# A two-layer decoder trunk: attention's transposes a slot later, logits in two banks, two steps held back at a chunk's end, the first microseconds in another order

## The chip, the cores and the metric

One core of a Trainium2 chip runs the whole program. The metric is the device time of one execution in microseconds (us). The kernel before was timed in three runs, and one more execution was profiled. The engines are TensorE (PE: matmuls and transposes, results in PSUM banks), VectorE (DVE), ScalarE (ACT), GpSimd (POOL) and SyncE (SP, which here only starts transfers).

## The reference

A batch of one, 256 tokens of width 2048, two layers, all in float32. Layer 0 is HGRN2 (a gated linear recurrence over chunks of 64 tokens), layer 1 native sparse attention (NSA) with 16 heads of 128 in 4 groups:

```python
for i in range(2):                       # x: (1, 256, 2048)
    h = rms_norm(x, g[i])
    x = x + (hgrn2_mixer(h) if i == 0 else nsa_mixer(h))
return rms_norm(x, final_gain)

# nsa_mixer, per group of 4 heads:
proj = h @ w_in                          # q, six of k and v, gate logits, z
K_cmp, V_cmp = compress_kv(...)          # 15 blocks of 32 tokens, stride 16
o = sum over b in (compressed, selected, window) of
        gate_b * softmax(q @ K_b.T + rel_bias) @ V_b
return (o * silu(z)) @ w_out
```

With 256 tokens every selection block is taken, so the selected and the window branch both see all causal keys. A head's logits for 256 queries cover 2 x 256 such keys and 15 compressed ones, for each half of the queries as far as the mask lets them.

## The kernel before, in words

**Products.** Each large product is split: an operand is cast to a rounded part `hi` (ACT, L132) and a rest `lo` (DVE, L142), and hi x hi, hi x lo and lo x hi are summed in PSUM. Weights come in pieces of 128x1024 on SP's queue into six buffers. The list `plan` holds all pieces in order, and `flush` goes through it; a chunk is a run of eight pieces whose products end in the same four PSUM banks (`mainps`). One piece is called a *slot* here: eight pairs of L173 (512 columns) and L175 (256 columns) on PE. Four more banks (`auxps`) serve everything else. At a chunk's end `take` (`gather`) copies each bank by ACT (L301) and adds its second half by DVE (L303); the next chunk's first product waits for its bank.

**Steps beside the products.** Everything else is a generator in the list `steps`. `flush` advances each of them twice a piece: once ahead of the piece's products (even steps) and once behind them (odd steps). So a step's place in the table `turns` decides where its instructions stand in each engine's queue, and each engine takes its queue in order.

**Attention.** The chunks of the NSA layer are q0, q1, q2, z0, q3, z1, z2, z3, after keys and values, and then the output product. `attend(g)` for the heads of group g starts 12g+2 slots behind q0. In a head it does: `logits` (nine matmuls on PE, Kh and Kl against qh and ql), `biased` (DVE adds the bias and takes the maxima), `exps` (ACT, with sums), `weigh` (reciprocal on DVE, scaling on ACT and DVE), `transposes` (PE, seven, in two banks), `evacuate` (ACT casts to `ph` and `pc`, DVE forms `pl`), and for every two heads `values` (PE, in two halves) and `values_out` (ACT, `ot`). `gated` multiplies z by its norm, applies SiLU (ACT, which loads a table before and after), multiplies by the attention's output and splits it into `yh` (ACT) and `yl` (DVE).

**Start.** `load_x` and `emit_load` start the loads of x and the first weights on SP. `split_x` transposes two tiles of x (PE, L326) and splits them (ACT L329, DVE L332). `setup` makes masks and tables a step at a time; its transposes of the parameter rows `prow` (L392) feed the lower bounds of the gates, which the first chunk's end needs.

Of the kernel before, what the change touches and what calls it, by code (L numbers as in the profile page):

```python
# [8 lines left out]
F32 = mybir.dt.float32  # L9
# [7 lines left out]
P = 128  # L17
# [28 lines left out]
def kernel(ctx: ExitStack, tc: tile.TileContext, x, norm_gains, final_gain, rel_bias,  # L46
# [19 lines left out]
    def aux_bank():  # L66
        return psa.tile([P, 512], F32, tag="aux", name="auxps")
# [172 lines left out]
    def start_piece(i):  # L240
        while state["hi"] <= min(i, len(plan) - 1):
            j = state["hi"]
            ch, kts, _ = plan[j]
            if ch and ch["before"]:
                ch["before"](kts)
            prefetch(j, 1)
            while state["lo"] <= j:
                emit_lo(state["lo"])
                state["lo"] += 1
            prefetch(j, 0)  # L250

    def flush():
        start_piece(2)
        finished = None
        for i, (ch, kts, last) in enumerate(plan):
            starting = ch is not None and ch["before"]
            if ch is not None:
                if finished:
                    finished()
                    finished = None  # L260
                advance()
            if not starting:
                prefetch(i, SPLIT_AHEAD)
            if ch is None:
                continue
            emit_products(i, (lambda: start_piece(i + 3)) if starting else None)
            if last and ch.get("take"):
                ch["take"](ch["ps"])
# [38 lines left out]

    sp = ctxs["start"].enter_context(tc.tile_pool(name="start", bufs=1))
    xt = sp.tile([P, 2, D], F32, name="xt")
    ssqp = sp.tile([P, 2, 4], F32, name="ssqp")  # L310
    ssq = sp.tile([P, 2], F32, name="ssq")
    junk = sp.tile([P, 512], F32, name="junk")
# [35 lines left out]
    brow = const.tile([NH, 384], F32, name="brow")  # L348
    rb = sp.tile([BUCKETS, NH], F32, name="rb")

    def setup():

        si = sp.tile([P, 32], I32, name="si")
# [22 lines left out]
        nc.vector.tensor_tensor(gt, ti, si, op=ALU.is_ge)  # L376
        xf = sp.tile([P, 32], F32, name="xf")
        nc.gpsimd.tensor_copy(xf, xi)
        yield
        yield  # L380
        cg = sp.tile([P, 7, 32], F32, name="cg")
# [2 lines left out]
        mf = sp.tile([P, 6, 32], F32, name="mf")  # L384
        nc.vector.tensor_sub(mf, cg[:, 0:6], cg[:, 1:7])
        nc.gpsimd.tensor_copy(masks, mf)
        yield
        yield
        yield
        pp = aux_bank()  # L390
        for i in range(2):
            nc.tensor.transpose(pp[:, i * P:(i + 1) * P], prow[:, i, :], ident)  # L392
# [468 lines left out]
    def attend(g):  # L861
# [4 lines left out]

        def logits(h):

            b0, b1, b2 = aux_bank(), aux_bank(), aux_bank()
            ks = [t[:, g] for t in NS["K"]]  # L870
            first = [bass.AP(tensor=k.tensor, offset=k.offset, ap=[list(k.ap[0]), [280, 2], [1, 136]]) for k in ks]
            for tt, dst, (kh, kl) in ((0, b0[:, 0:272], first), (1, b1[:, 0:272], [k[:, 8:280] for k in ks]),
                                      (1, b2[:, 0:256], [k[:, 280:536] for k in ks])):
                qh, ql = (t[:, h % 2, tt * P:(tt + 1) * P] for t in NS["q", g, h // 2])
                mm3(dst, qh, ql, kh, kl, True, True)
            l = ns.tile([P, 816], F32, tag="L", name="L", bufs=1)
            mx = ns.tile([P, 6], F32, tag="mx", name="mx")
# [4 lines left out]
            prt = ((1, b0[:, 8:136], bi[:, 128:256], l[:, 0:128]),  # L882
                   (0, b0[:, 0:7], bi[:, 159:256:16], l[:, 256:263]),
                   (2, b0[:, 136:264], bi[:, 128:256], l[:, 128:256]),
                   (4, b1[:, 0:256], bi, l[:, 304:560]),
                   (3, b1[:, 256:271], bi[:, 31:256:16], l[:, 288:303]),
                   (5, b2[:, 0:256], bi, l[:, 560:816]))
            L[h] = l, sm, prt, mx

        def biased(h):  # L890
# [75 lines left out]
        def at(slot, after, f, *a):  # L966
            turns.setdefault(2 * slot + after, []).append((f, a))

        for h in range(4):
            at(3 * h, 1, logits, h)  # L970
            at(3 * h + 1, 0, biased, h)
            at(3 * h + 1, 1, exps, h)
            at(3 * h + 2, 0, weigh, h)
            at(3 * h + 2, 1, transposes, h)
            at(3 * h + 3, 0, evacuate, h)
        for a in range(2):
            at(6 + 6 * a, 1, values, a, 0)
            at(7 + 6 * a, 1, values, a, 1)
            at(8 + 6 * a, 0, values_out, a)
        if g + 1 < G:  # L980
            for a in range(2):
                at(10, 0, get_bias, g + 1, a)
        for n in range(max(turns) + 1):
            for f, a in turns.get(n, ()):
                f(*a)
            yield

# [120 lines left out]
    residual(("x1", 4), x1_dram, *cols[4])()  # L1108

    nc.gpsimd.memset(prow, 0.0)  # L1110
    nc.gpsimd.dma_start(prow[0:48, 0, :], hgrn_lb.rearrange("a (h d) -> (a h) d", d=HD))
    nc.gpsimd.dma_start(prow[48:49, 0, :], hgrn_head_gain)
    nc.gpsimd.dma_start(prow[49:50, 0, :], phi_k_b1)
    nc.gpsimd.dma_start(prow[50:51, 0, :], phi_v_b1)
    nc.gpsimd.dma_start(prow[0:32, 1, :], nsa_pe_k[0])
    nc.gpsimd.dma_start(prow[32:64, 1, :], nsa_pe_v[0])
    nc.gpsimd.dma_start(rb, rel_bias)
    for c in range(8):
        load_x(c)
        for i in ((0, 1) if c == 0 else (c + 1,)):  # L1120
# [1 line left out]
                loaded[i] = emit_load(i)  # L1122
    state["load"] = RAW_BUFS
    gp = aux_bank()
    nc.tensor.transpose(gp[:, :32], gn, ident[:32, :32])
    nc.vector.tensor_copy(gcol, gp[:, :32])
    start_piece(0)
    for i in range(10):
        nc.tensor.transpose(gp[:, 256:256 + P], ident, ident)
    run(setup())  # L1130
    run(norm_x())
    flush()
# [32 lines left out]
```

## Time and profile before

| | us |
|---|---|
| median of 3 runs (lowest, highest) | 987.43 (986.7, 988.48) |
| the profiled execution | 988.16 |
| its span, first to last instruction | 986.3 |
| PE busy | 968.3 (98% of the span) |
| DVE busy | 658.1 (67%) |
| ACT busy | 543.7 (55%) |
| POOL busy | 52.4 (5%) |

The span is what the trace shows; the 1.9 us between it and the profiled execution's time lie around the first and the last instruction. The mean granted TensorE clock is 0.998. A busy time is a sum over the whole span; where an engine waits, and for whom, is read stretch by stretch.

### The profile page before, as it was taken

To read this page: it belongs to the slowest core of one execution; us is meant where nothing else is said; L and a number is where in the kernel's file an instruction comes from. 1 tells how busy PE (TensorE), PEld (TensorE's weight loads), DVE (VectorE), ACT (ScalarE), POOL (GpSimd) and SP (SyncE) were. 2 spreads that over 40 slices of the span, in tenths; PEclk is the share of its full clock that TensorE was granted. 3 is DMA by queue.
4 is the path that set the end of the run, shared out by engine and by line. 5 is a ranking of instruction groups with operands and counts; after the bars stand their busy time and mean duration, and the time that the engine had idled before them with its cause. 6 is when DMAs were issued, how large, how long until landed. Compare 5 with 4: busy or idle time off the path is not lost.

```text
span 986.3 us, 17479 instructions
## 1 busy us (share of the span) xinstructions
PE 968.3 (98%) x6721; PEld 836.3 (85%) x6721; DVE 658.1 (67%) x1274; ACT 543.7 (55%) x976; POOL 52.4 (5%) x154
## 2 busy tenths in 40 slices
PE   7999999999999999999999999999999999999996
PEld 6888888888888887888888898998899889888886
DVE  5778376846784678365556766455787888786654
ACT  6734563446344634455545655445777877875442
POOL 3101000100010001000011000000000000000000
PEclk9999999999999999999999999999999999999999
DMA  9555565555556555667777666574454445457662
GB/s 316 179 162 174 159 190 152 171 170 176 166 158 186 165 165 154 201 186 243 236 223 227 197 213 192 165 242 162 138 162 130 149 129 151 149 164 239 204 214 98
DMA packets 102612, 178.98 MB, mean 181 GB/s; under 512 B 6016, under 2 KB 25056, under 8 KB 102400
## 3 DMA queue, kind: packets, MB, share of 16 engines
q1 hardware_dynamic: 100512, 171.86, 56.8%
q0 software_dynamic: 1680, 5.46, 1.7%
q8 instruction: 53, 0.87, 0.4%
q10 hardware_dynamic: 336, 0.54, 0.1%
q14 instruction: 31, 0.25, 0.1%
HBM read 173.62 MB, written 4.22 MB: 180 GB/s over the span
## 4 chain that ended last, share of the span: by engine, by line
PE 92%; ACT 3%; DVE 2%; issue 1%; DMA 1%; SPq 0%; POOL 0%; DVEq 0%; POOLq 0%; ACTq 0%
PE mainps L150 40%; PE mainps L173 28%; PE mainps L175 14%; PE auxps L150 4%; PE auxps L491 2%; ACT L L900 1%; DVE lo L142 1%; DMA xt<-in_x_dram 1%; ACT hi L132 1%; PE auxps L920 1%; PE auxps L326 0%; PE auxps L502 0%; PE auxps L549 0%; PE auxps L550 0%; PE auxps L506 0%
## 5 line engine op out<-in xcount | busy, mean ns | idle before, releaser
L132 ACT CAST hi<-raw 128x1024 fp32r<-128x1024 f32 (+3 forms) x317 | 328.6, 1040 | 288.7 <-PE mainps L150 176.2
L142 DVE TENSOR_TENSOR lo<-raw,hi 128x1024 fp32r<-128x1024 f32 (+3 forms) x317 | 380.1, 1208 | 160.4 <-ACT hi L132 158.8
L173 PE MATMUL mainps<-xx,hi 128*128 128x512 f32 x1280 | 455.3, 398 | 4.1 <-DVE zs L303 3.2
L175 PE MATMUL mainps<-xx,lo 128*128 128x256 f32 x1280 | 357.6, 279 | 0.0
L173 PEld LDWEIGHTS mainps<-xx,hi 128*128 128x128 f32 x1280 | 240.8, 188 | 59.1 <-DVE zs L303 4.1
L175 PEld LDWEIGHTS mainps<-xx,lo 128*128 128x128 f32 x1280 | 241.8, 189 | 0.2
L150 PE MATMUL mainps<-hi,xx 128*128 128x512 f32 (+1 forms) x704 | 211.8, 377 | 0.0
L150 PEld LDWEIGHTS mainps<-hi,xx 128*128 128x128 f32 x704 | 128.4, 188 | 23.2
L150 PE MATMUL mainps<-lo,xx 128*128 128x512 f32 (+1 forms) x352 | 130.8, 372 | 0.0
L150 PE MATMUL mainps<-hi,yh 128*128 128x512 f32 (+1 forms) x288 | 105.9, 368 | 0.0
L150 PE MATMUL mainps<-hi,yl 128*128 128x512 f32 (+1 forms) x288 | 105.3, 366 | 0.0
L150 PE MATMUL mainps<-lo,yh 128*128 128x512 f32 (+1 forms) x288 | 105.3, 366 | 0.0
L150 PEld LDWEIGHTS mainps<-lo,xx 128*128 128x128 f32 x352 | 66.1, 188 | 10.1
L150 PEld LDWEIGHTS mainps<-hi,yl 128*128 128x128 f32 x288 | 54.3, 189 | 8.7
L150 PEld LDWEIGHTS mainps<-lo,yh 128*128 128x128 f32 x288 | 54.4, 189 | 8.6
L150 PEld LDWEIGHTS mainps<-hi,yh 128*128 128x128 f32 x288 | 54.4, 189 | 8.5
L900 ACT ACTIVATE L<-L,mx 128x128 f32<-128x128 f32 (+1 forms) x96 | 37.5, 393 | 23.4 <-DVE mx L895 23.4
L303 DVE TENSOR_TENSOR zs<-mainps,zs 128x256 f32<-128x256 f32 x48 | 18.7, 420 | 13.2 <-ACT zs L301 12.2
L533 POOL COPY ST<-S 32x128 f32<-32x128 f32 x32 | 14.6, 455 | 226.4 <-DVE S L526 225.2
L893 DVE CUSTOM_DVE_ANT_0 L<-auxps,bias 128x128 f32<-128x128 f32 (+1 forms) x96 | 22.0, 291 | 3.4 <-PE auxps L150 2.7
L938 DVE TENSOR_TENSOR pl<-auxps,ph 128x512 fp32r<-128x512 f32 (+1 forms) x32 | 17.3, 554 | 9.8 <-ACT ph L934 8.4
L564 DVE SCALAR_TENSOR_TENSOR y<-auxps,rs,sz 128x128 f32<-128x128 f32 x32 | 9.0, 344 | 22.2 <-POOL rs L79 22.2
(243 smaller groups left out, 859.3 us busy)
## 6 DMA issues: line engine op xcount, KB each, us to landing
raw<-in_hgrn_w_in_dram SPq DMA_DIRECT2D x127, 512.0 KB, 3.9
raw<-in_nsa_w_in_dram SPq DMA_DIRECT2D x104, 512.0 KB, 3.8
raw<-in_hgrn_w_out_dram SPq DMA_DIRECT2D x32, 512.0 KB, 4.8
raw<-in_nsa_w_out_dram SPq DMA_DIRECT2D x32, 512.0 KB, 4.4
raw<-in_nsa_w_in_dram SPq DMA_DIRECT2D x10, 420.0 KB, 3.4
xt<-in_x_dram SPq DMA_DIRECT2D x8, 256.0 KB, 8.4
raw<-in_x_dram SPq DMA_DIRECT2D x4, 512.0 KB, 4.0
x_dram<-x POOLq DMA_DIRECT2D x4, 512.0 KB, 6.2
```

What stands on the lines that cost most here:

```text
L132: nc.scalar.copy(hi[:, :m], raw[:, :m])
L142: nc.vector.tensor_sub(lo[:, :m], raw[:, :m], hi[:, :m].bitcast(F32))
L150: nc.tensor.matmul(dst, a, b, start=first and n == 0, stop=last and n == 2, skip_group_check=True)
L173: nc.tensor.matmul(ps, hv[:, fs], xx[:, k].rearrange("p a t -> p (a t)"), start=k == 0, stop=False, skip_group_check=True)
L175: nc.tensor.matmul(ps[:, S:], lv[:, fs], xh[:, k], start=False, stop=k == KT - 1, skip_group_check=True)
L303: nc.vector.tensor_add(o, p[:, :S], o)
L491: nc.tensor.matmul(dst[32 * b:32 * b + 32, i0 % 4:(i1 - 1) % 4 + 1, j, :], Kg[:, cs], QQ[:, q0:2, cs], start=True, stop=True, tile_positio ...
L533: nc.gpsimd.tensor_copy(ST[rs, :, 0:3:2, rs], S32[rs].rearrange("p (h t) c -> p h t c", h=2))
L893: nc.vector.tensor_tensor_reduce(out=dst, in0=lg, in1=b, op0=ALU.add, op1=ALU.max, scale=1.0, scalar=-3e38, accum_out=mx[:, i:i + 1])
L900: nc.scalar.activation(dst, dst, AF.Exp, bias=mx[:, i:i + 1], accum_out=sm[:, i:i + 1])
L920: nc.tensor.transpose(t1[:, i * P:(i + 1) * P], l[:, c0:c0 + P], ident)
L938: nc.vector.tensor_sub(pl[:, ks, hh, :], t, ph[:, ks, hh, :].bitcast(F32))
```

## The change

Two banks for a head's logits in place of three: the first takes 272 columns and then 16, the second 512. A head's transposes move from slot 3h+2 to 3h+3, directly ahead of the next head's logits; its evacuation moves to slot 3h+4 and stands first there. Both halves of `values` come in one step, at slot 8+6a behind the products, `values_out` a slot later, and the next group's bias (`get_bias`) behind the products of slot 10. In a chunk's last slot (`state["seam"]`) `biased` and `weigh` are held until behind `take`. `yl` follows `yh` by two steps in place of four.

At the start, `hi` and `lo` of piece 0 are formed ahead of `split_x`'s results, `flush` prepares one piece less ahead, the parameter rows are loaded behind POOL's `xf` in place of at the beginning, their transposes come one piece later, and of the transposes that keep PE busy seven multiplications of zeros now stand first and six behind the first `split_x`.

```diff
+            starting = ch and ch["before"]
+            if starting and j:
                 ch["before"](kts)
             prefetch(j, 1)
...
+            if starting and not j:
+                ch["before"](kts)
...
     def flush():
-        start_piece(2)
+        start_piece(1)
...
+            state["seam"] = ch is not None and last and bool(ch.get("take"))
...
-            emit_products(i, (lambda: start_piece(i + 3)) if starting else None)
+            emit_products(i, (lambda: start_piece(i + 2)) if starting else None)
...
     def setup():
...
         nc.gpsimd.tensor_copy(xf, xi)
+        load_parameters()
...
-        yield
-        yield
-        yield
+        for _ in range(5):
+            yield
         pp = aux_bank()
...
         def logits(h):
-            b0, b1, b2 = aux_bank(), aux_bank(), aux_bank()
+            b0, b1 = aux_bank(), aux_bank()
...
-            for tt, dst, (kh, kl) in ((0, b0[:, 0:272], first), (1, b1[:, 0:272], [k[:, 8:280] for k in ks]),
-                                      (1, b2[:, 0:256], [k[:, 280:536] for k in ks])):
+            for tt, dst, (kh, kl) in ((0, b0[:, 0:272], first), (1, b1, both),
+                                      (1, b0[:, 272:288], [k[:, 264:280] for k in ks])):
...
         for h in range(4):
-            at(3 * h, 1, logits, h)
             at(3 * h + 1, 0, biased, h)
             at(3 * h + 1, 1, exps, h)
             at(3 * h + 2, 0, weigh, h)
-            at(3 * h + 2, 1, transposes, h)
-            at(3 * h + 3, 0, evacuate, h)
-        for a in range(2):
-            at(6 + 6 * a, 1, values, a, 0)
-            at(7 + 6 * a, 1, values, a, 1)
-            at(8 + 6 * a, 0, values_out, a)
+            at(3 * h + 3, 1, transposes, h)
+            at(3 * h, 1, logits, h)
+            at(3 * h + 4, 0, evacuate, h)
+        for a in range(2):
+            for half in range(2):
+                at(8 + 6 * a, 1, values, a, half)
+            at(9 + 6 * a, 0, values_out, a)
...
+        late = (biased, weigh)
+        first_of = {evacuate: 0}
+        held = []
         for n in range(max(turns) + 1):
-            for f, a in turns.get(n, ()):
+            todo = sorted(turns.get(n, ()), key=lambda t: first_of.get(t[0], 1))
+            if n % 2 == 0 and state["seam"]:
+                held = [t for t in todo if t[0] in late]
+                todo = [t for t in todo if t[0] not in late]
+            elif n % 2:
+                todo, held = held + todo, []
+            for f, a in todo:
                 f(*a)
             yield
...
-        steps_between = (3, 2, 4) if g + 1 < G else (1, 2, 2)
+        steps_between = (3, 2, 2) if g + 1 < G else (1, 2, 2)
```

On PE, in the attention, a head's logits stand alone in the kernel before, behind a slot's last pair of products (a row is line, operation, output and inputs, size):

```order
L175 MATMUL mainps<-xx,lo 128x256
L150 MATMUL auxps<-Kh,qh 128x272
L150 MATMUL auxps<-Kl,qh 128x272
L150 MATMUL auxps<-Kh,ql 128x272
L150 MATMUL auxps<-Kh,qh 128x272
L150 MATMUL auxps<-Kl,qh 128x272
L150 MATMUL auxps<-Kh,ql 128x272
L150 MATMUL auxps<-Kh,qh 128x256
L150 MATMUL auxps<-Kl,qh 128x256
L150 MATMUL auxps<-Kh,ql 128x256
L173 MATMUL mainps<-xx,hi 128x512
```

On PE in the changed kernel the previous head's seven transposes (L936 to L939) stand directly ahead of them:

```order
L936 MATMUL auxps<-ident,L 128x128 x4
L938 MATMUL auxps<-ident,L 128x128 x2
L939 MATMUL auxps<-ident,L 47x128
L150 MATMUL auxps<-Kh,qh 128x272
L150 MATMUL auxps<-Kl,qh 128x272
L150 MATMUL auxps<-Kh,ql 128x272
L150 MATMUL auxps<-Kh,qh 128x512
L150 MATMUL auxps<-Kl,qh 128x512
L150 MATMUL auxps<-Kh,ql 128x512
L150 MATMUL auxps<-Kh,qh 128x16
L150 MATMUL auxps<-Kl,qh 128x16
L150 MATMUL auxps<-Kh,ql 128x16
```

What moved: the transposes by a slot, and the logits' widths from 272, 272 and 256 to 272, 512 and 16.

On ACT before, around the first SiLU of the attention (z0's, `zs`), the SiLU with its two table loads stands behind a head's evacuation (`ph`, `pc`):

```order
L909 ACTIVATE L<-L,sm 128x256 x2
L132 CAST hi<-raw 128x1024
L934 CAST ph<-auxps 128x4x128
L934 CAST ph<-auxps 128x2x128
L936 CAST pc<-auxps 15x128 x2
L132 CAST hi<-raw 128x1024
L1000 ACT_TABLE_LOAD
L1000 ACTIVATE zs<-zs 128x512 x2
L1003 ACT_TABLE_LOAD
L1003 ACTIVATE one<-one 128x1
L132 CAST hi<-raw 128x1024
```

On ACT after, at the same place, it stands ahead of the evacuation of group 1's last head:

```order
L925 ACTIVATE L<-L,sm 128x256 x2
L132 CAST hi<-raw 128x1024 x2
L1027 ACT_TABLE_LOAD
L1027 ACTIVATE zs<-zs 128x512 x2
L1030 ACT_TABLE_LOAD
L1030 ACTIVATE one<-one 128x1
L950 CAST ph<-auxps 128x4x128
L950 CAST ph<-auxps 128x2x128
L952 CAST pc<-auxps 15x128 x2
L132 CAST hi<-raw 128x1024
```

What moved: the evacuation, from two casts and the table loads ahead of the SiLU to directly behind it.

On PE at the program's beginning, before (L326 are the transposes of x, L1129 those that only keep PE busy):

```order
L1125 MATMUL auxps<-ident,gn 128x32
L326 MATMUL auxps<-ident,xt 128x128 x4
L1129 MATMUL auxps<-ident 128x128 x10
L326 MATMUL auxps<-ident,xt 128x128 x4
L173 MATMUL mainps<-xx,hi 128x512
L175 MATMUL mainps<-xx,lo 128x256
```

On PE at the beginning, after (L332 are the transposes of x, L1147 the multiplications that keep PE busy):

```order
L1147 MATMUL auxps<-zeros 128x128 x7
L1150 MATMUL auxps<-ident,gn 128x32
L332 MATMUL auxps<-ident,xt 128x128 x4
L1147 MATMUL auxps<-ident 128x128 x6
L173 MATMUL mainps<-xx,hi 128x512
L175 MATMUL mainps<-xx,lo 128x256
L173 MATMUL mainps<-xx,hi 128x512
L175 MATMUL mainps<-xx,lo 128x256
L332 MATMUL auxps<-ident,xt 128x128 x4
```

What moved: the first two pairs of products, from behind the second `split_x` to ahead of it.

## Rows read from the trace of the kernel before

**Rows 1.** The page's first part: busy time, share and instructions of each engine.

```profile
PE 968.3 (98%) x6721; PEld 836.3 (85%) x6721; DVE 658.1 (67%) x1274; ACT 543.7 (55%) x976; POOL 52.4 (5%) x154
```

**Rows 2.** Windows: length, busy time of each engine, PE clock, DMA share, GB/s.

```profile
680.00:870.00 190.00, 185.81 (x1178) 166.44 (x1177) 152.53 (x478) 146.79 (x384) 6.05 (x21) 1.00 0.47 142
950.00:986.30 36.30, 28.91 (x218) 27.69 (x217) 17.37 (x32) 11.07 (x17) 1.14 (x2) 0.94 0.35 120
```

**Rows 3.** Waits of PE over the whole span: total us, times, longest.

```profile
PE mainps L173 <- DVE zs L303: 3.2, 4, 1.7
PE auxps L920 <- DVE L L911: 1.0, 1, 1.0
PE mainps L173 <- DVE Kg L303: 0.7, 1, 0.7
```

**Rows 4.** Chain that ended last: start us, us, what.

```profile
61.07 2.75 PE mainps L150 x12
...
686.38 1.11 PE auxps L150 x9
...
703.29 0.44 PE auxps L920 x4
```

**Rows 5.** Timeline of PE at 565 us: start, us, engine, line, operation.

```profile
565.03 0.33 PE L798 MATMUL auxps<-scratch 128*128 128x64 f32 x2
...
565.48 0.28 PE L175 MATMUL mainps<-xx,lo 128*128 128x256 f32 x1
```

**Rows 6.** Timeline of PE around the seam q3|z1.

```profile
797.31 0.60 PE L920 MATMUL auxps<-ident,L 128*128 128x128 f32 x4
...
799.96 0.50 PE L173 MATMUL mainps<-xx,hi 128*128 128x512 f32 x1 [1.72 <-DVE zs L303]
```

**Rows 7.** Timeline of all engines from 774 to 790 us.

```profile
775.50 0.85 ACT L934 CAST ph<-auxps 128x512 fp32r<-128x512 f32 x2
...
776.11 1.25 DVE L938 TENSOR_TENSOR pl<-auxps,ph 128x512 fp32r<-128x512 f32 x2 [0.53 <-ACT ph L934]
...
777.99 1.28 ACT L1000 ACT_TABLE_LOAD   x1
...
778.29 1.23 DVE L142 TENSOR_TENSOR lo<-raw,hi 128x1024 fp32r<-128x1024 f32 x1
...
779.55 0.29 DVE L893 CUSTOM_DVE_ANT_0 L<-auxps,bias 128x128 f32<-128x128 f32 x1
...
781.04 1.22 DVE L142 TENSOR_TENSOR lo<-raw,hi 128x1024 fp32r<-128x1024 f32 x1
...
781.85 1.03 ACT L132 CAST hi<-raw 128x1024 fp32r<-128x1024 f32 x1
...
782.78 0.40 ACT L900 ACTIVATE L<-L,mx 128x128 f32<-128x128 f32 x1
...
785.24 0.59 ACT L962 COPY ot<-auxps 128x512 f32<-128x512 f32 x1
...
785.73 0.91 ACT L909 ACTIVATE L<-L,sm 128x256 f32<-128x256 f32 x2
...
789.03 1.14 ACT L1012 CAST yh<-zs 128x512 fp32r<-128x512 f32 x2
```

**Rows 8.** Timeline of all engines from 9 to 21 us.

```profile
9.81 0.78 PE L173 MATMUL mainps<-xx,hi 128*128 128x512 f32 x1
...
12.01 1.23 DVE L142 TENSOR_TENSOR lo<-raw,hi 128x1024 fp32r<-128x1024 f32 x1
...
15.10 0.39 PE L173 MATMUL mainps<-xx,hi 128*128 128x512 f32 x1
...
20.61 0.32 POOL L378 CAST xf<-xi 128x32 f32<-128x32 int32 x1 [12.66 <-DVE rowmask L372]
```

**Rows 9.** Transfers of the first 20 us: GB/s in half microseconds; an issue, KB, us to landing.

```profile
GB/s 0 0 0 14 205 284 364 346 362 199 216 172 220 297 330 369 314 371 382 362 363 350 363 340 342 375 363 369 389 373 373 352 369 381 367 391 377 389 381 385
...
rb<-in_rel_bias_dram POOLq DMA_DIRECT2D x1, 2.0 KB, 6.6
```

More of the change, by code (lines that the diff above doesn't have):

```diff
@@ L243, in start_piece @@
             ch, kts, _ = plan[j]
-            if ch and ch["before"]:
+            starting = ch and ch["before"]
+            if starting and j:
                 ch["before"](kts)
@@ L309 @@
     xt = sp.tile([P, 2, D], F32, name="xt")
+    zeros = sp.tile([P, P], F32, name="zeros")
+    nc.vector.memset(zeros, 0.0)
     ssqp = sp.tile([P, 2, 4], F32, name="ssqp")
@@ L349, with load_parameters @@
     rb = sp.tile([BUCKETS, NH], F32, name="rb")
+    def load_parameters():
+        nc.gpsimd.dma_start(prow[0:48, 0, :], hgrn_lb.rearrange("a (h d) -> (a h) d", d=HD))
+        nc.gpsimd.dma_start(prow[48:49, 0, :], hgrn_head_gain)
+        nc.gpsimd.dma_start(prow[49:50, 0, :], phi_k_b1)
+        nc.gpsimd.dma_start(prow[50:51, 0, :], phi_v_b1)
+        nc.gpsimd.dma_start(prow[0:32, 1, :], nsa_pe_k[0])
+        nc.gpsimd.dma_start(prow[32:64, 1, :], nsa_pe_v[0])
+        nc.gpsimd.dma_start(rb, rel_bias)
     def setup():
@@ L867, in logits @@
         def logits(h):
-            b0, b1, b2 = aux_bank(), aux_bank(), aux_bank()
+            b0, b1 = aux_bank(), aux_bank()
             ks = [t[:, g] for t in NS["K"]]
             first = [bass.AP(tensor=k.tensor, offset=k.offset, ap=[list(k.ap[0]), [280, 2], [1, 136]]) for k in ks]
-            for tt, dst, (kh, kl) in ((0, b0[:, 0:272], first), (1, b1[:, 0:272], [k[:, 8:280] for k in ks]),
-                                      (1, b2[:, 0:256], [k[:, 280:536] for k in ks])):
+            both = [bass.AP(tensor=k.tensor, offset=k[:, 8:].offset, ap=[list(k.ap[0]), [272, 2], [1, 256]]) for k in ks]
+            for tt, dst, (kh, kl) in ((0, b0[:, 0:272], first), (1, b1, both),
+                                      (1, b0[:, 272:288], [k[:, 264:280] for k in ks])):
                 qh, ql = (t[:, h % 2, tt * P:(tt + 1) * P] for t in NS["q", g, h // 2])
@@ L884, in logits @@
                    (2, b0[:, 136:264], bi[:, 128:256], l[:, 128:256]),
+                   (3, b0[:, 272:287], bi[:, 31:256:16], l[:, 288:303]),
                    (4, b1[:, 0:256], bi, l[:, 304:560]),
-                   (3, b1[:, 256:271], bi[:, 31:256:16], l[:, 288:303]),
-                   (5, b2[:, 0:256], bi, l[:, 560:816]))
+                   (5, b1[:, 256:512], bi, l[:, 560:816]))
             L[h] = l, sm, prt, mx
@@ L973, in attend @@
             at(3 * h + 2, 0, weigh, h)
-            at(3 * h + 2, 1, transposes, h)
-            at(3 * h + 3, 0, evacuate, h)
+            at(3 * h + 3, 1, transposes, h)
+            at(3 * h, 1, logits, h)
+            at(3 * h + 4, 0, evacuate, h)
         for a in range(2):
-            at(6 + 6 * a, 1, values, a, 0)
-            at(7 + 6 * a, 1, values, a, 1)
-            at(8 + 6 * a, 0, values_out, a)
+            for half in range(2):
+                at(8 + 6 * a, 1, values, a, half)
+            at(9 + 6 * a, 0, values_out, a)
         if g + 1 < G:
             for a in range(2):
-                at(10, 0, get_bias, g + 1, a)
+                at(10, 1, get_bias, g + 1, a)
+        late = (biased, weigh)
+        first_of = {evacuate: 0}
+        held = []
         for n in range(max(turns) + 1):
-            for f, a in turns.get(n, ()):
+            todo = sorted(turns.get(n, ()), key=lambda t: first_of.get(t[0], 1))
[5 more added lines that the diff above has]
+            for f, a in todo:
                 f(*a)
@@ L1110 @@
     nc.gpsimd.memset(prow, 0.0)
[L1111 to L1117, printed above, removed]
     for c in range(8):
@@ L1124, with keep_busy @@
     gp = aux_bank()
+    def keep_busy(n, m):
+        for _ in range(n):
+            nc.tensor.matmul(gp[:, 256:256 + P], m, m, start=True, stop=True)
+    keep_busy(7, zeros)
     nc.tensor.transpose(gp[:, :32], gn, ident[:32, :32])
@@ L1127 @@
     start_piece(0)
-    for i in range(10):
-        nc.tensor.transpose(gp[:, 256:256 + P], ident, ident)
+    keep_busy(6, ident)
     run(setup())
```

## The prediction

> **What bounds the kernel now.** I read the page's table of engines first: TensorE (PE) is busy 968.3 us of a span of 986.3 [rows 1], so only what adds or removes PE work, or makes PE wait, can move the time. The windows by stretch say where it waits: of the 190 us from 680 to 870, in which the attention runs between the NSA projections, 185.81 are busy, so 4.19 us are lost there; the tail from 950 on loses 7.4 us, and the change leaves the tail alone [rows 2]. The table of waits names the attention's: 3.2 us in four waits of a new chunk's first product for its bank (`zs` gathered on VectorE, DVE), the longest 1.7, and 1.0 us of transposes waiting for the weights `L` [rows 3]. ScalarE (ACT) and DVE are not the bound as a whole, but in this stretch each wait ends with one of them. So the reader is to watch three things: PE's own work in the attention, the lateness of ACT against PE there, and the first 40 us.
>
> **1. The logits' matmuls: +4.5 us.** Before, a head's nine logits matmuls (272, 272 and 256 columns, three each) take 1.11 us, so about 0.124, 0.124 and 0.117 each. Matmuls of 512 columns come 12 in 2.75 us, 0.229 each [rows 4]. After, the nine have 272, 512 and 16 columns. The same keys are covered; only the cut differs, so by columns nothing would be lost. What matters is a 16-column matmul, which this trace does not have. The bounds: by columns it would take 16/256 of 0.117, so 0.007; by its neighbours of 256 columns at most 0.117. The nearest row is a pair of matmuls of 64 columns at 565.03: from its start to that of the row two further on are 0.45 us (565.03 to 565.48), in which one L173 of 0.23 (512 columns) also runs, so 0.11 each, as much as 256 columns cost [rows 5]. Four times fewer columns saved 6%, so something other than columns sets the pace at that size, and I take 0.111. Then a head costs 3 x 0.124 + 3 x 0.229 + 3 x 0.111 = 1.39, which is 0.28 more; for 16 heads **+4.5 us** (bounds -0.5 at 0.007 and +4.8 at 0.117). PE has no cover: it is itself the bound.
>
> The Trainium skill weighs in on both sides, in "TensorE: Matmul & The Clock Gate". Its section "Back-to-back issue gap" has an issue floor of about 25 ns for matmuls of 1 to 64 columns; by that alone the sum would be about +0.4 (an estimate). Its section "LDWEIGHTS (loading the stationary operand)" gives a load of P/1.2 ns, about 107 for 128 columns of weights, and each of these matmuls has weights of its own; by that it would be +4.3 (an estimate). The trace's 0.11 goes with the second.
>
> **2. The attention's waits: +4.2 us.** What moves: a head's transposes go from slot 3h+2 to 3h+3 (a slot is one weight piece, eight pairs of L173 and L175), directly ahead of the next logits, and its evacuation from 3h+3 to 3h+4, ahead of the next head's biased logits. That gives the weights one slot more, but it lines up ACT's and DVE's work for one head in a row. From the start e of an evacuation on ACT: the first half of `ph` takes 0.6, then DVE's `pl` and `pc` 2.2 (776.11 to 778.29), then the biased logits 1.5 (779.55 to 781.04) [rows 7], so the exponentials start at e + 4.4; they take 2.45 (782.78 to 785.24), the reciprocal and the weighing on ACT 1.3 more (0.4 from their end to DVE's reciprocal and back, 0.9 for the two), so the weights stand at about e + 8.1. With two casts `hi` of 1.0 each, ACT comes round in 10.1. PE comes round in three slots (3 x 2.77) and 2.05 of transposes and logits, 10.4, or 12.8 where values lie between. So the loop has nearly no slack, where before DVE could do the biased logits without waiting for the evacuation. Each extra on ACT now makes the next step late: the SiLU with its two table loads 3.86 (777.99 to 781.85), `yh` 1.1, `ot` 0.5 [rows 7].
>
> The place where it costs most is the seam q3|z1, where before PE waits longest: the transposes at 797.31 run behind the chunk's last product, and the next product starts at 799.96 [rows 6]. In the new order on ACT the SiLU stands ahead of group 1's last evacuation. From the evacuation before it to this one ACT needs 6.85 (evacuation to the end of the exponentials), 1.3, 2.0 (two casts) and 3.86: 14.0, where PE needs 10.4; it is 3.6 late. From there to group 2's first evacuation it needs 6.85, 1.3, 2.0 and 1.55 (`ot`, `yh`), so 11.7, where PE needs 12.8 with the values: 2.5 late. From that evacuation the gather of the chunk still has 6.85, one cast 1.0, its own copy 0.4 and DVE's add 0.4 ahead of it, 8.65, while PE has the logits (1.39) and two slots (5.54), 6.93. So PE waits 1.7 + 2.5, some 4.0, instead of 1.7: **+2.3**. Held back at the seam are only biased logits and weights, which does not help, as the exponentials of the head before stand ahead of the gather.
>
> At q1|q2 the transposes that run behind the last product (0.44 and three more, about 0.7) [rows 4] go a slot later, so PE waits that much longer: **+0.7**. In z2 the transposes wait for a head that is late by the SiLU: e + 8.1 with 3.6 of lateness against 10.4, about 2.0 where it was 1.0: **+1.0**. In z3 the same lateness meets the values, which now come both halves in one step: I take **+0.5** (between 0 and 1.5). z0|q3 is covered by the logits and gives back 0.3. Sum +4.2, so 8.4 us idle in place of 4.19. Bounds: -3.7 (all but 0.5 gone) and +6.
>
> **3. The start: -2.1 us.** Before, PE waits for the second part of x and transposes it; piece 0's first product comes at 9.81, piece 2 at 15.10 [rows 8]. After, piece 0's first half stands ahead of those transposes and runs while x is on its way. At the pace of before, transposes end at 9.8, the rest of piece 0 and piece 1 take about 2.8, and piece 2 could begin at 12.6, but its `lo` ends on DVE at 13.24 (12.01 + 1.23) [rows 8]: piece 2 at about 13.0, -2.1. In addition the seven parameter transfers leave POOL's queue at this time. The transfer rate falls from some 360 to 172 to 220 GB/s between 4.5 and 6.5 us, while they are under way; that is some 350 KB short, 1.0 us [rows 9]. With x a microsecond earlier the gain is 3.1. I take 3.2 less a term on the other side: the parameters' transposes come a piece later, so the chain behind them (copies, the lower bounds, the squares' sum, the gather) ends nearer to the first chunk's end, where PE waits 0.7 already [rows 3]. A piece is 2.8 us and the chain was some 0.7 too long before; between 0 and 2.8 I take 1.1. Their transfers, now behind POOL's cast `xf` (at 20.61 before [rows 8], sooner by the start's gain after), take 6.6 us from issue to landing [rows 9], so they land at 27 to 29, about when their transposes come; I put nothing on that here and a rival below. Net **-2.1** (-3.2 to +0.5).
>
> SP's queue, the order of the weight loads and both projections outside the attention stay as they are, at nothing; the 13 warming matmuls stand in PE's idle time ahead of 9 us.
>
> **Sum.** 4.5 + 4.2 - 2.1 = +6.6 us. Against the profiled execution (988.16, 1.9 around its span) that would be 994.8; it stands 0.7 over the median 987.43, on which I put the forecast: **994.0 us**.
>
> **The rivals.** A measurement of this kernel tells 0.2%, about 2 us, from no change.
> - *ACT keeps up* (the other side). If the evacuations start with their transposes, PE waits for the gather at q3|z1 no longer than the held-back steps spare, and nearly all of the 4.19 goes. For it: ACT is busy only 146.79 of the 190 us [rows 2], and the weights have a slot more. Against it: 10.1 of 10.4 with 5.4 of extras a group. It decides if group 2's first evacuation starts no later than 0.8 us after its transposes end and the exponentials of that head end before the chunk's last product. Then -3.7, +4.5, and with the first seam unhurt -3.2: **985.0**.
> - *Short matmuls are cheap*: a 16-column matmul at 0.03 or less gives +0.6 in place of 4.5, so **990.1**. For it: columns set the pace elsewhere; against it the 64-column row.
> - *The waits only move*: no change in their sum, +4.5 - 2.1, **989.8**.
> - *The parameters land late*: POOL issues them behind `xf`, and a microsecond or two of lateness at the parameters' transposes stalls PE: +1.5, **995.5**.
> - *The clock falls* in a wait of 4 us. The only stretch where the granted clock reads under 1.00 is the tail at 0.94, where PE idles 7.4 of 36.3 us [rows 2]; behind the 1.7 wait the attention's stretch still reads 1.00, the level of 2.4 GHz. Price: the kernel's first products take 0.78 where later ones take 0.39 [rows 8]; a wait's worth of products at that rate is some 1.5 to 2, **995.8**. The Trainium skill's "TensorE: Matmul & The Clock Gate", section "Why this matters for your kernels", warns that idle gaps between bursts of matmuls bring the lower clock back; the waits of before in the attention do not show it.
>
> **How the numbers follow.** My forecast 0.42; ACT keeps up 0.18; cheap matmuls 0.12; waits only move 0.12; late parameters 0.08; clock 0.08. The range 985 to 998 leaves out what is faster than the second case and the upper bounds together (4.8 + 6 + 0.5); the forecast's own range is 991.5 to 996.5. Faster takes the second case and a mixture of cheap matmuls and few waits; the fourth lies at the edge of "same": faster 0.19, same 0.15, slower 0.66.
>
> **What would show it.** Right: 16-column matmuls 0.11 apart; a wait of about 4 us at the seam q3|z1 with the SiLU ahead of an evacuation; the first product near 6.5 and piece 2 near 12 to 13; more wait at the first chunk's end. Wrong: the three short matmuls in under 0.1 together, the idle time of the stretch below 4.19, or the first 40 us no shorter.

## The result, and the profile after

The changed kernel takes 998.42 us (median of 4 runs, 996.51 to 999.13) against 987.82 for the kernel before in the same comparisons: a ratio of 1.0103, interval [1.0088, 1.0118], so some 10.2 us slower (the medians are 10.6 apart). The forecast was 994.0, 6.6 slower, and its range reached to 998.0: the median lies 0.4 beyond that, the ratio put on the 987.43 of the forecast (997.6) just within. The sign was right, and so were the places in the attention; the start's gain did not come, and the size is a third too small.

The profiled execution of the changed kernel spans 996.4 us, 10.1 more than before. The page's first part and PE's waits over the whole span (us, times, longest) answer to [rows 1] and [rows 3]:

```profile
PE 978.4 (98%) x6737; PEld 843.7 (85%) x6737; DVE 658.3 (66%) x1275; ACT 543.7 (55%) x976; POOL 52.2 (5%) x154
```

```profile
PE mainps L173 <- DVE zs L307: 5.0, 2, 3.6
PE mainps L173 <- DVE Kg L307: 2.1, 1, 2.1
PE mainps L175 <- DVE lo L142: 1.9, 1, 1.9
PE auxps L1147 <- DVE zeros L315: 1.1, 1, 1.1
```

PE's busy time rose by 10.1 us, as much as the span. That alone would say "more work on PE", and it misleads: the waits also grew, and what made room for them lies ahead of 9 us, where PE now warms up instead of waiting. The waits in the attention went from 4.2 us in five waits to 7.0 in three, those at the first chunk's end from 0.7 to 2.1. The busy time holds something else as well. The windows show it (the columns of [rows 2]; the third number from the right is the granted clock):

```profile
36.00:38.00 2.00, 1.01 (x3) 0.92 (x4) 1.42 (x4) 1.89 (x5) 1.92 (x5) 0.70 0.79 240
38.00:40.00 2.00, 2.00 (x7) 1.71 (x7) 1.23 (x1) 1.19 (x2) 1.08 (x3) 0.50 0.11 28
680.00:870.00 190.00, 182.99 (x1115) 162.26 (x1114) 143.21 (x449) 138.58 (x361) 5.93 (x20) 0.98 0.45 134
804.00:806.00 2.00, 1.67 (x6) 1.44 (x7) 1.93 (x9) 0.99 (x4) 0.00 (x0) 0.70 0.93 313
806.00:808.00 2.00, 2.00 (x9) 1.71 (x8) 2.00 (x6) 1.50 (x3) 0.00 (x0) 0.50 0.45 165
856.00:858.00 2.00, 2.00 (x8) 1.71 (x8) 0.78 (x5) 1.48 (x7) 0.00 (x0) 0.50 0.53 132
```

Three times, behind the waits of 2.1, 3.6 and 1.9 us, the granted clock reads 0.50, the level of 1.2 GHz. PE is "busy" all of 38 to 40 us, but with 7 matmuls where 13 or 14 are usual. That lasts 3 to 4 us each time. Such a stretch is called a slow stretch from here on.

To keep start and attention apart, two distances are taken from each trace: when the first matmul of the recurrence (QQ, Kg) starts, and how long it is from the first logits matmul to the end of the last matmul.

| kernel | first QQ, us | first logits to end, us | against before (ratio, interval) |
|---|---|---|---|
| before | 63.79 | 292.69 | 1 |
| changed | 63.87 | 302.68 | 1.0103 [1.0088, 1.0118] |
| attention_only | 63.09 | 303.65 | 1.0103 [1.0088, 1.0118] |
| start_only | 64.32 | 292.67 | 1.0005 [0.9995, 1.0014] |
| start_early_params | 62.41 | 292.71 | 1.0001 [0.9991, 1.0011] |
| start_squares | 63.23 | 292.71 | 1.0020 [1.0008, 1.0032] |
| start_freed | 61.44 | 292.50 | 0.9989 [0.9980, 0.9998] |
| logits_cut | 65.15 | 296.46 | 1.0047 [1.0029, 1.0064] |
| wide_cut | 62.69 | 293.32 | 1.0009 [0.9996, 1.0021] |
| fill_waits | 62.86 | 300.92 | 1.0075 [1.0058, 1.0093] |
| biased_first | 62.00 | 298.26 | 1.0052 [1.0032, 1.0072] |
| no_silu_z0 | 62.72 | 298.64 | 1.0049 [1.0031, 1.0067] |
| no_hold | 62.69 | 309.54 | 1.0163 [1.0137, 1.0188] |
| attention_mended | 64.04 | 294.99 | 1.0018 [1.0009, 1.0027] |

So all of the loss is in the attention, +10.0 us. Its column is firm: the five kernels with the attention of before read 292.5 to 292.7. The column of the first QQ matmul is not. Five rows have the start of before unchanged (before, attention_only, logits_cut, wide_cut, attention_mended), and they read 62.7 to 65.2; five have the new start unchanged, and they read 63.9 and 64.3 where a slow stretch follows the first chunk's end (changed, start_only) and 62.0 to 62.7 where none does (biased_first, no_silu_z0, no_hold). So one trace does not tell a microsecond there, and what the start is worth has to come from runs.

### The profile page after: what moved, and what is told of

Same layout as the page of the kernel before. It is cut to its first block, busy times and chain, and to the rows that moved or that the text cites. A ratio compares the mean times of both kernels' runs of the same rounds, so it can differ in the third digit from the quotient of the medians.

```text
span 996.4 us, 17505 instructions
## 1 busy us (share of the span) xinstructions
PE 978.4 (98%) x6737; PEld 843.7 (85%) x6737; DVE 658.3 (66%) x1275; ACT 543.7 (55%) x976; POOL 52.2 (5%) x154
## 4 chain that ended last, share of the span: by engine, by line
PE 90%; ACT 5%; DVE 3%; issue 1%; DMA 0%; POOL 0%; POOLq 0%; DVEq 0%; ACTq 0%
PE mainps L150 40%; PE mainps L173 26%; PE mainps L175 13%; PE auxps L150 4%; PE auxps L506 2%; ACT hi L132 1%; ACT L L916 1%; DVE lo L142 1%; DVE L L909 1%; PE auxps L936 1%; ACT ph L950 0%; PE auxps L1147 0%; PE auxps L517 0%; DMA raw<-in_hgrn_w_in_dram 0%; PE auxps L565 0%
## 5 line engine op out<-in xcount | busy, mean ns | idle before, releaser
L150 PEld LDWEIGHTS mainps<-lo,xx 128*128 128x128 f32 x352 | 66.1, 188 | 10.1
```

The lines of the kernel that those rows point to most:

```text
L150: nc.tensor.matmul(dst, a, b, start=first and n == 0, stop=last and n == 2, skip_group_check=True)
```

## The experiments

**Start or attention?** Two kernels, each with half of the change: *attention_only* is the changed kernel with the start's edits taken back, *start_only* the kernel before with them.

> The changed kernel with the start of before. If start and attention add up and the start's net is nothing, it is as slow as the changed kernel, about 10 us over before: some 4 for the short matmuls, 2 for more waiting and 3.7 for two stretches at half speed behind waits of 3.6 and 1.9 us. If the start were a gain of 2 to 3 hidden by the attention, it would be 12 to 13 over before.

> The kernel before with only the new start (the attention is that of before). If the changed kernel's start gains 2.9 us up to the end of the first chunk, loses 1.4 in the wait there and 1.5 in the half-speed products behind that wait, the time stays within 0.5 us of before, with a wait near 2.1 us at the first chunk's end and a granted clock of 0.5 behind it. If the start is a clean gain and all of the loss is in the attention, it is 2 to 3 us faster.

attention_only is as slow as the changed kernel, start_only within a microsecond of the kernel before: 0.5 us slower by ten runs (-0.5 to 1.4). Within that, the halves add up, and neither hides the other. (The 1.0 us that attention_only's trace has over the changed kernel's goes with the slow stretch behind its seam q3|z1, which lasts twice as long in that execution.) In start_only PE waits 2.1 us at the first chunk's end, as expected, and its clock falls to 0.50 in 40 to 42 us:

```profile
40.00:42.00 2.00, 2.00 (x9) 1.81 (x8) 0.00 (x0) 0.57 (x1) 0.00 (x0) 0.50 0.50 113
```

**The short matmuls.** *logits_cut* is the kernel before with only the new cut, *wide_cut* the same with another cut for the same two banks:

```diff
 # logits_cut
+(0, b0[:, 0:272], first), (1, b1, both), (1, b0[:, 272:288], [k[:, 264:280] for k in ks])
 # wide_cut
+(0, b0[:, 0:272], first), (1, b0[:, 272:512], [k[:, 8:248] for k in ks]), (1, b1[:, 0:288], [k[:, 248:536] for k in ks])
...
+nc.vector.tensor_tensor(mx[:, 4:5], mx[:, 4:5], mx[:, 6:7], op=ALU.max)
```

> The kernel before with only the new cut of the logits (272, 512 and 16 columns in two banks). If a short matmul costs a weight load, as the trace of the changed kernel suggests (27, 112 and 112 ns for the three), a head's logits take 1.33 us in place of 1.11 and the kernel is 3.5 to 4.5 us slower, about 991.5. If short matmuls are cheap and the changed kernel's loss lies in its waits, it is within 1 us of before. If two banks in place of three make the logits wait less for a free bank, a part of the cost is given back and the waits for the weights L shrink.

> The kernel before with the logits in two banks, cut at 272, 240 and 288 columns (16 of the selected keys' logits in the second bank; VectorE takes a seventh maximum and joins two). If what made the cut at 272, 512 and 16 dear is only that a matmul of 16 columns takes as long as its weights' load, this costs PE 1.10 us a head as before, and the kernel is within 0.5 us of before where the other cut lost 4.6. If two banks themselves cost, by waits for a free bank or by the order of the heads, it is slower by the same 4 to 5 us; if a matmul under 256 columns is slow in itself, by 1 to 10 us.

logits_cut loses 4.6 us by its runs (2.9 to 6.3), 3.8 by its trace from the first logits on; wide_cut's interval ends at 0.2%, and its trace from the first logits on is 0.6 us longer. Both have two banks, the same heads in the same order and the same products, so the short matmuls cost it and not the banks. The timeline of the changed kernel shows how (PEld are the weights' loads):

```profile
687.17 0.39 PE L150 MATMUL auxps<-Kh,ql 128*128 128x512 f32 x1
...
687.41 0.17 PE L150 MATMUL auxps<-Kh,qh 128*128 128x16 f32 x1
687.41 0.19 PEld L150 LDWEIGHTS auxps<-Kl,qh 128*128 128x128 f32 x1
687.43 0.26 PE L150 MATMUL auxps<-Kl,qh 128*128 128x16 f32 x1
687.52 0.19 PEld L150 LDWEIGHTS auxps<-Kh,ql 128*128 128x128 f32 x1
687.54 0.26 PE L150 MATMUL auxps<-Kh,ql 128*128 128x16 f32 x1
687.63 0.19 PEld L173 LDWEIGHTS mainps<-xx,hi 128*128 128x128 f32 x1
687.66 0.49 PE L173 MATMUL mainps<-xx,hi 128*128 128x512 f32 x1
...
687.98 0.28 PE L175 MATMUL mainps<-xx,lo 128*128 128x256 f32 x1
```

The same place in the kernel before, behind a logits matmul of 256 columns:

```profile
687.33 0.39 PE L173 MATMUL mainps<-xx,hi 128*128 128x512 f32 x1
687.56 0.28 PE L175 MATMUL mainps<-xx,lo 128*128 128x256 f32 x1
```

The loads come 0.11 us apart and the matmuls behind them too; only from the first short one to the second it is 0.026 to 0.031, in all 16 heads. The three matmuls of 16 columns take 0.25 us together, where three of 272 or 256 columns take 0.36. What the first one seems to save comes back behind the third: the next product starts 0.32 us ahead of its successor, where 0.23 is usual (687.66 to 687.98, against 687.33 to 687.56 before). So the three cost 0.34 a head, three loads' worth. In logits_cut all distances from one matmul's start to the next's, from the first logits on and without the waits, add up to 4.4 us more than before; its waits there are 0.6 shorter (3.6 against 4.2), which leaves the trace's 3.8. The Trainium skill, "TensorE: Matmul & The Clock Gate", section "LDWEIGHTS (loading the stationary operand)", gives about 107 ns for 128 columns of weights; the 0.11 here agrees. Its floor of about 25 ns in "Back-to-back issue gap" agrees with the one gap of 0.03, but it does not set the pace where each matmul has weights of its own.

**The slow stretches.** *fill_waits* is the changed kernel with idle transposes in three waits:

```diff
+    def fill(n):
+        for b in (aux_bank(), aux_bank()):
+            for _ in range(n):
+                nc.tensor.transpose(b[:, :P], ident, ident)
...
+        fills = {ends[0]: 7, ends[-4]: 14, ends[-2] - 4: 6}
...
+            if i in fills:
+                fill(fills[i])
```

> The changed kernel with idle transposes on TensorE in the three places where it waits before the slow stretches: 14 at the first chunk's end, 28 at the seam q3|z1, 12 ahead of the products in z2 that wait for lo (0.11 us each, so 1.5, 3.1 and 1.3 us, less than each wait). They compute nothing that is used. If the waits cost a second time because the clock falls behind them, the granted clock stays at 1.00 and the kernel is some 5 us faster than the changed one (about 993.5), with the waits as long as they were. If the slow products have another cause, it is as slow as the changed kernel or slower.

The clock stays at 1.00, as the windows of fill_waits show at the same three places:

```profile
38.00:40.00 2.00, 2.00 (x14) 1.72 (x13) 1.23 (x1) 1.25 (x2) 1.13 (x3) 1.00 0.08 23
...
806.00:808.00 2.00, 2.00 (x17) 1.89 (x16) 2.00 (x3) 1.61 (x4) 0.11 (x1) 1.00 0.24 91
856.00:858.00 2.00, 2.00 (x16) 1.90 (x15) 2.00 (x6) 2.00 (x5) 0.12 (x1) 1.00 0.41 157
```

The gather comes no earlier: at the seam its timeline has the idle transposes and then the first product, 118.0 us behind the first logits as in the changed kernel (there 804.33):

```profile
800.00 3.22 PE L258 MATMUL auxps<-ident 128*128 128x128 f32 x28
803.90 0.50 PE L173 MATMUL mainps<-xx,hi 128*128 128x512 f32 x1 [0.68 <-DVE zs L316]
```

But of the 5 us expected it gives back 2.6 (995.8 against 998.4 by the medians; 1.8 in the attention by the traces). Some of the rest meets a new wait: with full speed behind the seam PE comes to z3 earlier, ScalarE and DVE are as late as before, and PE waits there 0.65 us for a `lo` that it did not wait for when it was slow. So the lower clock costs some 5 us of products and 2 to 3 us of time. Of the three places, the two in the attention carry this: at the first chunk's end the same wait was followed by a slow stretch in only two of the five executions without idle transposes.

**What makes ScalarE late.** *no_silu_z0* leaves out one SiLU, *biased_first* changes the order on DVE, *no_hold* takes the hold away:

```diff
 # no_silu_z0
+        if g:
             for a in range(2):
                 nc.scalar.activation(zs[a], zs[a], AF.Silu)
-        if g + 1 < G:
+        if 0 < g and g + 1 < G:
             nc.scalar.activation(NS["one"], NS["one"], AF.Exp, scale=0.0)
 # biased_first
-        first_of = {evacuate: 0}
+        first_of = {biased: 0}
 # no_hold
-            state["seam"] = ch is not None and last and bool(ch.get("take"))
+            state["seam"] = ch is not None and last and bool(ch.get("take")) and False
```

> The changed kernel without the SiLU of group 0's gate and its two table loads (so the output of group 0 is not gated by it). If these 3.9 us on ScalarE ahead of the evacuation set the wait at q3|z1, as the sum in the prediction has it, the wait falls from 3.6 us to between 0.5 and 2, its slow stretch goes, and the kernel is 3 to 5 us faster than the changed one; the wait in z2, behind another SiLU, stays. If the wait comes from something else (the order on VectorE, the gather itself), it stays over 3 us.

> The changed kernel with one word changed: in a slot the biased logits stand first on VectorE and the evacuation behind them. If ScalarE is late because its exponentials wait for the evacuation and the biased logits one behind the other (4.4 us), each head gains 1.4 to 2 us on ScalarE, the wait at q3|z1 falls from 3.6 to under 1.5, that in z2 vanishes, no slow stretch follows, and the kernel is 4 to 7 us faster than the changed one. If the SiLU's 3.9 us alone makes ScalarE late, the wait stays over 2.5 us and the time within 2 us of the changed kernel.

> The changed kernel without the hold: in a chunk's last slot the biased logits and the weighing stand ahead of the gather again. At q1|q2 and q3|z1 the weighing takes 0.9 us on ScalarE and, behind the reciprocal, 0.8 on VectorE. If the hold spares the gather that, both waits grow by 0.8 to 1.5 us and the kernel is 1.5 to 3 us slower than the changed one. If, as the prediction says, the hold does not help because the exponentials stand ahead of the gather in any case, it is within 1 us of the changed kernel.

Without the SiLU the wait at q3|z1 falls from 3.6 to 1.4 us, no slow stretch follows it, and the wait in z2 behind the next SiLU stays. The kernel is 5.3 us faster than the changed one (993.1), a little more than expected. PE's waits in no_silu_z0:

```profile
PE mainps L173 <- DVE zs L307: 2.8, 2, 1.4
PE mainps L175 <- DVE lo L142: 2.1, 2, 2.0
```

biased_first gives back about 5 us, too. PE's waits in it:

```profile
PE mainps L173 <- DVE zs L307: 2.9, 2, 2.2
...
PE mainps L175 <- DVE lo L142: 0.6, 2, 0.5
```

The wait in z2 shrank to 0.5, that at q1|q2 halved, and 2.2 us stayed at q3|z1, more than expected, with a slow stretch behind it that was not expected either:

```profile
803.00:805.00 2.00, 2.00 (x8) 1.63 (x6) 2.00 (x7) 1.83 (x3) 0.00 (x0) 0.50 0.80 256
```

Both causes are real, then: the order on DVE makes each round long, and the SiLU on ScalarE comes on top. The hold was misjudged: without it the waits for the gather grow from 5.0 to 10.7 us, and the kernel is 6 us slower still (1004.3), twice what was expected:

```profile
PE mainps L173 <- DVE zs L307: 10.7, 4, 5.1
```

**What is left with both repairs.** *attention_mended* is attention_only with the wide cut and biased first.

> The start of before, and the changed attention (transposes a slot later, both halves of the values in one step, the seam's steps held) with two repairs: the wide cut of the logits (272, 240 and 288 columns) and the biased logits ahead of the evacuation on VectorE. If the short matmuls, the order on VectorE and the clock behind long waits are all that made the changed attention slow, it is within 1.5 us of before (the biased order gave 5.0 back and the cut 4.6 of 10.2). If the later transposes themselves make ScalarE late, waits over 2 us stay at q3|z1 and it is 2 us or more slower than before.

It comes to 1.8 us (0.9 to 2.7) over before, between its two cases (within 1.5, or 2 and more), and the sign of the second is there: one long wait is left, at q3|z1, with its slow stretch behind it:

```profile
PE mainps L173 <- DVE zs L304: 4.1, 4, 3.0
```

There ScalarE is busy without a gap from 789.6 us to the gather's end. So no version of the changed attention that was run beats that of before, even without the short matmuls: with a whole slot more for the weights, the gather of q3 still follows a round that the SiLU stands in. That it is the transposes' later slot, and not the joined values or the steps held back, is argued from the chain; no run moves the transposes alone.

**The first chunk's end.** Three kernels with the attention of before. *start_early_params* is start_only with the parameters loaded and transposed as before, *start_squares* takes the later squares one a step as well, *start_freed* adds two edits to that (the squares' sums in memory of their own, and the lower bounds two steps earlier):

```diff
+    ssqp = const.tile([P, 2, 4], F32, name="ssqp")
+    ssq = const.tile([P, 2], F32, name="ssq")
...
         nc.vector.tensor_copy(brow[:, HD - 1:HD - 1 + 256], pp[:NH, 256:512])
-        yield
...
         nc.vector.tensor_sub(lbe, lb3, lbm[:, None, :].to_broadcast([P, 3, NH]))
-        yield
```

> The new start, but the parameter rows loaded at the program's beginning and transposed a piece earlier, as before; the attention is that of before. If the late parameters cause the wait at the first chunk's end, it shrinks from 2.1 to below 1 us, the clock stays at 1.00 and the kernel is 2 us or more faster than before. If the wait comes from the squares' sum or the weights, or if the early transfers hold up x as much as the start gains, it is no faster than the new start alone.

> The new start with early parameters, and the squares of the later half of x one a step in place of every second step, so that their sum is there two pieces earlier; the attention is that of before. If the first chunk's end then waits because ScalarE's squares come last (sum at 35.65 us, gather at 36.12), the wait of 2.5 us falls to 1.5 or less and the kernel is 1 to 1.5 us faster than the start with early parameters alone. If ScalarE's casts, or the weights on their way, come last, it stays.

> The attention of before, and the new start with early parameters, with three edits against the wait at the first chunk's end: the squares of x's later half one a step, the lower bounds in the step in which their rows are copied, and the squares' sums (ssqp, ssq) kept in memory of their own. The gather's tiles Kg lie in the memory that the start's tiles leave, so ScalarE's copy must follow their last reader, which is POOL's rstd reading ssq (rstd ends at 36.1 us and the copy starts at 36.11 in both starts measured). If that reuse is what holds the gather, the copy no longer follows rstd, the wait falls from 2.5 us to under 1.2, and the kernel is 2 to 3 us faster than before. If the copy is held by the products or the casts ahead of it, the wait stays above 2 us and the time within 0.5 us of before.

The first two missed: the wait at the first chunk's end is 2.5 and 2.9 us, not shorter. start_squares is 2 us slower than before by its runs, which its trace does not explain. A hint is on record: seven of its ten runs have a mean clock of 0.995 or 0.996 and take 990.2 to 992.1 us, three have 0.997 and take 988.2 to 989.1, the traced one (988.7) among them. A slow stretch behind its long wait in most executions would fit; no trace shows one. What the two had in common with the changed kernel is this (timeline of the changed kernel at 34 to 37 us):

```profile
34.58 0.28 PE L175 MATMUL mainps<-xx,lo 128*128 128x256 f32 x1
...
35.64 0.15 DVE L350 TENSOR_REDUCE ssq<-ssqp 128x2 f32<-128x8 f32 x1
35.89 0.19 POOL L78 TENSOR_SCALAR rstd<-ssq 128x2 f32<-128x2 f32 x1 [14.22 <-DVE ssq L350]
36.11 1.20 ACT L305 COPY Kg<-mainps 128x256 f32<-128x256 f32 x4 [2.02 <-POOL rstd L78]
...
36.99 0.79 PE L173 MATMUL mainps<-xx,hi 128*128 128x512 f32 x1 [2.13 <-DVE Kg L307]
```

The copy of the products does not use `rstd`. It waits for it because its tiles lie where `ssq` was, as start_freed shows. start_early_params has the sum at the same time, 35.65, though its lower bounds are ready a microsecond earlier: there DVE makes a `lo` first. In start_squares the sum comes half a microsecond earlier, but `rstd` takes 1.08 us in place of 0.19. With `ssq` in memory of its own the copy starts ahead of the squares' sum (timeline of start_freed):

```profile
33.62 1.01 ACT L304 COPY Kg<-mainps 128x256 f32<-128x256 f32 x3
...
33.94 0.15 DVE L350 TENSOR_REDUCE ssq<-ssqp 128x2 f32<-128x8 f32 x1
...
34.20 1.08 POOL L78 TENSOR_SCALAR rstd<-ssq 128x2 f32<-128x2 f32 x1 [12.43 <-DVE ssq L350]
...
35.15 1.08 DVE L306 TENSOR_TENSOR Kg<-mainps,Kg 128x256 f32<-128x256 f32 x3
...
35.62 0.51 PE L173 MATMUL mainps<-xx,hi 128*128 128x512 f32 x1 [0.71 <-DVE Kg L306]
```

The wait is 0.7 us again. But the sum itself comes earlier here, too: `rstd` ends 0.4 us behind the chunk's last product, in start_squares 2.0 behind it. Had the copy still followed it (35.28), PE would have waited some 1.3 us (an estimate from these rows: a copy of 0.4 and an add of 0.45 behind it). So of the 2.2 us between 2.9 and 0.7 some 0.6 are the memory's, and the rest is the earlier sum's; no run has the one edit without the other. start_freed is the one version that beats the kernel before, by 1.1 us (0.2 to 2.0). Its first QQ matmul at 61.4 is earlier than in any execution with the start of before, by 1.3 to 3.7 us.

## Why the prediction was right, and where it was too small

**The short matmuls: right.** 4.5 us were forecast; logits_cut shows 4.4 of longer distances in its trace and 4.6 by its runs. The 64-column pair of [rows 5] was the right neighbour, read over the product behind it as well. The term counted three loads a head, and three it is: 0.25 us for the three matmuls and 0.09 at the product behind them.

**The attention's waits: right in place, 2.8 us in place of 4.2.** The chain of waits of the changed kernel is the sum of the prediction, step by step, from the SiLU to the gather (start, us, engine, tile, line):

```profile
779.82 1.28 ACT L1027
781.11 1.15 ACT zs L1027 x2
...
783.79 0.86 ACT ph L950 x2
...
788.29 2.45 ACT L L916 x12
...
793.71 1.04 ACT yh L1039 x2
...
795.70 0.76 ACT ph L950 x2
...
801.32 1.17 ACT L L916 x5
802.49 0.94 ACT hi L132
803.45 0.38 ACT zs L305
803.85 0.44 DVE zs L307
...
850.34 0.75 ACT ph L950 x2
...
854.57 1.14 DVE lo L142
```

From the first evacuation to the second are 11.9 us (11.7 forecast), from there to the gather's first copy 7.75 (7.85 forecast), and PE's wait is 3.6 where "some 4.0" stood (the terms there, 1.7 and 2.5, add up to 4.2). At q1|q2 it is 1.4 us, 0.5 more than before, where 0.7 more was forecast; z0|q3 gave its 0.3 back. In z2 the wait has the forecast length, 1.9, but not the forecast end: PE does not wait for the transposes' weights but for a `lo`, which stands behind the late evacuation and the biased logits on DVE. In z3 no wait followed, where 0.5 was put. The step that failed here is the sentence that the hold does not help: it spares 6 us (no_hold).

**The start: -2.1 forecast, nothing measured beyond noise (start_only, 0.5 us slower, -0.5 to 1.4).** The first half worked: the chunk's last product ends some 2.8 us earlier (34.9 against 37.7; over the executions 34.5 to 35.2 against 36.2 to 38.7). About 1.3 of that is pace and not order: before, the first two products start 0.57 us apart, in the changed kernel 0.33, though the granted clock reads 1.00 in both. It is so in four of the five executions with the start of before and in none of the nine with the new one. The prediction put the 13 warming matmuls at nothing; whether they do it was not tested. The term on the other side was mis-sized, 1.1 for the longer wait at the first chunk's end where the trace has 1.4, and its cause was right in part only: the parameters' lateness is not needed (with them early the wait is 2.5), the squares' sum is, and the gather follows it because of the reuse of the start's memory. The slow products behind the wait took the rest, where they came: in two of five executions. The parameters landed in time; PE has no wait at their transposes.

**The clock: the step that made the forecast too small.** It stood as a rival with 0.08, argued from a wait of 1.7 us that had left the clock at 1.00. The forecast itself put a wait of 4.0 us and one of 2.0 into the program and kept the clock at 1.00 in its own sum. The runs show three slow stretches, 5 us of products in this execution, 2.6 us of time by fill_waits. The rival's price, 1.5 to 2 us, fits one stretch; it counted one, not three.

The trace divides the 10.0 us from the first logits on so: 2.8 are longer waits; 3.1 are the two slow stretches there (22 products in 7.1 us, where at the usual distance they take 4.0); the 4.1 that are left are the longer distances of all other matmuls, which is the short matmuls' term (4.4 in logits_cut). So the forecast's errors had both signs: it was 1.4 too high on the waits and 0.4 on the short matmuls, and too low by some 2 on the start and by 3.1 on the clock. That they cancelled in part is luck.

## What to carry to other kernels

Don't cut a matmul so that a short one is left over when each has weights of its own: a balanced cut (272, 240 and 288 columns here) costs what its columns cost, a rest of 16 costs a load, part of which shows only at the matmul behind it. Before a gain is read from one trace, look how far traces of the same code lie apart: at this start it was 2.5 us. Where a change puts a wait of some two microseconds or more on PE, give products at half speed behind it a term of their own (here they followed nine of nine such waits in the attention and two of seven at the first chunk's end), and test with idle matmuls what of that is real. Before a wait at a handover is put down to the data, look for the instruction that releases it: if it is the last reader of a pool that was closed there, moving a small tile out of that pool lets the handover go ahead of it.

## What the runs showed of the hardware

The clock's fall does not go by the length of the wait alone. In the attention each wait of 1.94 us or more was followed by a stretch at 0.50 (nine waits from 1.94 to 5.1 us, in six kernels; those that idle transposes filled are not counted) and none of 1.91 or less; at the first chunk's end waits of 2.1 us were followed by one in the changed kernel and in start_only and by none in biased_first, no_silu_z0 and no_hold, and neither were those of 2.5 and 2.9 us in start_early_params and start_squares. Nor does it come at once: in start_only the products run at full pace for 1.4 us behind the wait and only then take twice as long. The Trainium skill, "TensorE: Matmul & The Clock Gate", section "Why this matters for your kernels", warns that idle gaps between bursts bring the lower clock back; the attention's rows agree, and the start's show waits as long that do not.
